# A hybrid decoder layer on one core: sums over a head's features, from float32 products to float32r products in two parts

## The chip, the core and the metric

The kernel runs on one core of one Trainium2 chip. The metric is device microseconds of one execution; lower is better. Before the change the median of three runs is 2262.58 us (2262.24 to 2262.78). Engines are named as in the profile: PE multiplies matrices and PEld is its weight load, DVE is the vector engine, ACT the scalar engine, POOL is GpSimd, and SP issues DMAs.

## The reference

One decoder layer on 256 tokens with 2048 features: a SwiGLU feed-forward block, a mixer, cross-attention to a memory, a second feed-forward block and a last norm. The mixer runs a sliding-window attention beside an RWKV-7 time mix of 16 heads with 64 features each, and merges them behind gates. The change touches three places of the time mix, each a sum or mean over the 64 features of a head:

```python
kk = k * k_k
kk = kk / jnp.maximum(jnp.sqrt(jnp.sum(kk * kk, axis=-1, keepdims=True)), 1e-12)   # 1
k = k * (1.0 + (a - 1.0) * k_a)
y = rwkv7_scan(r, decay, k, v, -kk, kk * a)
mean = jnp.mean(y, axis=-1, keepdims=True)
var = jnp.mean(jnp.square(y - mean), axis=-1, keepdims=True)                       # 3
y = ((y - mean) * lax.rsqrt(var + GN_EPS)).reshape(B, T, RWKV_WIDTH)
y = y * ln_w + ln_b
bonus = jnp.sum(r * k * r_k, axis=-1, keepdims=True) * v                           # 2
y = (y + bonus.reshape(B, T, RWKV_WIDTH)) * g
```

Everything is float32 in the reference, with the projections as plain products (`p = h @ w_in`, `y_attn @ w_proj_attn` and so on).

## The kernel before

**The weight stream.** The large products read 2048-feature weights in tiles of two k-tiles by 512 columns. SP issues their loads (`load`, L331) into the ring `raw` of four buffers. `split_unit` makes two float32r halves of a tile: ACT casts it to `hi` (L339) and DVE subtracts to get `lo` (L340), in rings of three. `times` (L412, L413, L414) then multiplies the activations' halves with them: high by hi, high by lo, low by hi, all float32r, accumulating in PSUM (`acc`). Such a tile with both token halves is an item: twelve products of 128x512. `next_item` splits items ahead of their use (AHEAD = 2).

**The work between.** Other work is written as generators, and an `Interleave` called `bg` advances them. `product` calls `bg.tick()` after each token half of an item, so there are two ticks an item. A tick advances the first generators of each group by one `yield`: const, feat, attn (two at once), ew (one at a time), chain (three), norm (one), mem. `idle(n)` yields n times. The time mix's steps are in these groups:

- `removal_keys(h)`, group ew, for each half h of the 16 heads: `kk`, its square `sq` (ACT, L1000), two products with `bdones` (L1005), square root (L1006), bound and reciprocal on DVE, then `kk` and `at` scaled. From these come 64-row products `kk` with `at` (L1042), in two groups c of eight, with the two row halves e in turn, each half into a PSUM bank of its own; DVE masks them to `lt` (L1048), POOL writes `lt` to a DRAM scratch `ld` (L1053).
- `substitute()`, group ew, behind both: SP reads `ld` back as `dl` in four transfers (L1063), and DVE solves a triangular system in small steps, `tmp` (L1070) and `xt` (L1075).
- `receptances(h)` and `values(h)`, group ew, later: the first forms the product r·k·r_k in `kt`; the second multiplies it with `bdones` (two products, L1131) for the bonus.
- `pair(h, j)`, group chain: the recurrence, for two heads at once.
- `finish(h, i)`, group norm, four in all: the square of `y`, a product with `bdmean` (L1273), square root (L1274), reciprocal, the group norm's scale and the gate.

`bdones` and `bdmean` are 128x128 float32 with two 64x64 blocks of 1 and of 1/64 on the diagonal, so that one product sums over the features of both heads in a tile and spreads the sum back over them. POOL makes them with memsets at the start of the mixer (L209 to L215). The sums go to PSUM banks `tr` (two).

**Around the change.** While `removal_keys` and `substitute` run, the foreground is four rounds of two products, w_in for a gate and then w_proj_attn (`ga`): ACT takes the sigmoid of the gate from PSUM (L1092), DVE multiplies the projection into it (L1095). During `receptances`, `values`, `pair` and `finish` the foreground is w_in for r and v and for the second gate, and then w_proj_rwkv.

**Memory and order.** The mixer's tiles of 4 KB for each partition come from one ring, `t4`, of N4 = 20 buffers; a tile that takes a buffer waits for the last use of the one before it. The instructions stand in each engine's queue in the order of the built program, which is not always the order of the source: a step whose operand comes late can stand behind later ones.

Of the kernel before, what the change touches and what calls it, by code (L numbers as in the profile page):

```python
# [8 lines left out]
F32R = mybir.dt.float32r  # L9
AF = mybir.ActivationFunctionType  # L10
ALU = mybir.AluOpType
# [4 lines left out]
P = 128  # L16
T = 256
# [12 lines left out]

UP, DOWN = 2.0**40, 2.0**-40
GROUPS = ((0, 4), (4, 4), (8, 3))
N4 = 20

AHEAD, LOADED = 2, 4

# [96 lines left out]
def decoder_layer(ctx: ExitStack, tc: tile.TileContext, a: dict, out: bass.AP):  # L133
    nc = tc.nc
    act, dve, pool, pe = nc.scalar, nc.vector, nc.gpsimd, nc.tensor
# [16 lines left out]
    def f32(x):  # L152
        return x.bitcast(F32)
# [7 lines left out]
    def tr():  # L161
        return ps.tile([P, 512], F32, tag="tr", name="tr", bufs=2)
# [5 lines left out]
    def idle(n):  # L168
        for _ in range(n):
            yield  # L170
# [20 lines left out]
    def mixer_constants(sp):  # L191

        abias = sp.tile([P, 2, P], F32, name="abias")
        pool.memset(abias[:], 0.0)
        select(abias[:, 0, :], abias[:, 0, :], [[1, P]], ALU.is_gt, NEG, 0, -1)
        select(abias[:, 1, :], abias[:, 1, :], [[-1, P]], ALU.is_ge, NEG, 0, 1)

        ups = sp.tile([P, 2, P], F32, name="ups")[:, 0, :]
        pool.memset(ups, UP)
        mask3 = sp.tile([P, 3, P], F32, name="mask3")  # L200
        select(mask3[:, 0, :], ups, [[1, P]], ALU.is_gt, 0.0, 0, -1)
        select(mask3[:, 1, :], ups, [[1, P]], ALU.is_ge, 0.0, 0, -1)
        select(mask3[:, 2, :], ups, [[1, P]], ALU.is_ge, 0.0, 0, -1)

        mask_l = sp.tile([P, P], F32, name="mask_l")
        select(mask_l[:], ups, [[-1, P]], ALU.is_gt, 0.0, 0, 1)
        bdones = sp.tile([P, P], F32, name="bdones")
        bdmean = sp.tile([P, P], F32, name="bdmean")
        pool.memset(bdones[:], 0.0)  # L209
        pool.memset(bdmean[:], 0.0)  # L210
        pool.memset(bdup, 0.0)
        for e in range(2):
            q = slice(64 * e, 64 * e + 64)
            pool.memset(bdones[q, q], 1.0)
            pool.memset(bdmean[q, q], 1.0 / 64)  # L215
            pool.memset(bdup[q, q], UP)
        pool.tensor_tensor(center[:], ident[:], bdmean[:], ALU.subtract)
        keep = sp.tile([P, 2, P], F32, name="keep")
        pool.memset(keep[:], 1.0)
        pool.memset(keep[:, :, 0:1], 0.0)  # L220
        return abias, mask3, mask_l, bdones, bdmean, keep

    sinks = cpool.tile([P, 16], F32, name="sinks")

# [41 lines left out]
    v = flat(a["rwkv_mu"])  # L266
# [462 lines left out]
    def aligned(sp):  # L729

        sp.tile([P, 16], F32, name="shift")
# [34 lines left out]

    with tc.tile_pool(name="mx", bufs=1, reuse_waits="tile") as sp:
        aligned(sp)
        abias, mask3, mask_l, bdones, bdmean, keep = mixer_constants(sp)

        def t4(name, shape=(P, 4, T), dt=F32):
            return sp.tile(list(shape), dt, tag="t4", name=name, bufs=N4)

# [10 lines left out]
            return s  # L784

        C4 = [0, P, 2 * P, 3 * P]


        def to_features(tok, dst, name):
            for q in (0, 2):  # L790
                act.copy(dst[:, q : q + 2, :], feat(tok, C4[q : q + 2]))
                yield
# [196 lines left out]
        kt = []  # L989

        def removal_keys(h):
            yield from wait_for(f"k{h}")
            yield from wait_for("decay")
            ei = cs[h]
            kk, sq = t4("kk"), t4("sq")
            for i in range(4):
                c = 4 * h + i
                act.activation(kk[:, i, :], kt[h][:, i, :], AF.Copy, scale=nk_k[:, c : c + 1])
            yield
            act.activation(sq[:], kk[:], AF.Square)  # L1000
            yield
            for i in (0, 2):
                b = tr()
                sq2 = sq[:, i : i + 2, :].rearrange("p c t -> p (c t)")
                pe.matmul(b[:], bdones[:], sq2, start=True, stop=True)  # L1005
                act.activation(sq2, b[:], AF.Sqrt)  # L1006
                yield
                dve.tensor_scalar(sq2, sq2, 1e-12, None, ALU.max)
                for k in range(2):
                    dve.reciprocal(sq[:, i + k, :], sq[:, i + k, :])  # L1010
                    yield from idle(2)
            dve.tensor_tensor(kk[:], kk[:], sq[:], ALU.mult)
            yield
            at_.append(t4("at"))
            for later, before in ((slice(1, P), ee[h][:, :, : P - 1]), (0, e0[h][:])):
                dve.scalar_tensor_tensor(
                    halves(at_[h])[:, :, later], halves(kk)[:, :, later], DOWN, before,
                    ALU.mult, ALU.mult,
                )
            yield  # L1020
            dve.scalar_tensor_tensor(kk[:], kk[:], -1.0, aa[h][:], ALU.mult, ALU.mult)
            yield
            dve.tensor_tensor(kk[:], kk[:], ei[:], ALU.mult)
            bt.append(kk)
            yield
            for i in range(4):
                c = 4 * h + i
                dve.tensor_scalar(
                    aa[h][:, i, :], aa[h][:, i, :], k_a[:, c : c + 1], ok_a[:, c : c + 1],
                    ALU.mult, ALU.add,  # L1030
                )
            pool.tensor_tensor(kt[h][:], kt[h][:], aa[h][:], ALU.mult)
            pool.tensor_tensor(aa[h][:], kt[h][:], ei[:], ALU.mult)

            for c in range(2):
                cs_ = slice(c * P, (c + 1) * P)
                lt = t4("lt", (P, 8, P))
                b = [mm() for _ in range(2)]
                for j in range(4):
                    for e in range(2):  # L1040
                        r = slice(64 * e, 64 * e + 64)
                        pe.matmul(  # L1042
                            b[e][:, j * P : (j + 1) * P], at_[h][r, j, cs_], bt[h][r, j, cs_],
                            start=True, stop=True,
                        )
                yield
                for e in range(2):
                    dve.tensor_tensor(  # L1048
                        lt[:, 4 * e : 4 * e + 4, :], b[e][:].rearrange("p (j s) -> p j s", j=4),
                        mask_l[:].unsqueeze(1).to_broadcast([P, 4, P]), ALU.mult,  # L1050
                    )
                o = h * 16 + c * 8
                pool.dma_start(ld[:, o : o + 8, :], lt[:])  # L1053
                yield
            yield
# [40 lines left out]
            pool.dma_start(blk(md, n), g[:])  # L1096


        rt, vtok, bv = [], [], []

        def receptances(h):
            yield from wait_for(f"r{h}")
            for i in range(4):
                c = 4 * h + i
                dve.scalar_tensor_tensor(
                    kt[h][:, i, :], rt[h][:, i, :], r_k[:, c : c + 1], kt[h][:, i, :],
                    ALU.mult, ALU.mult,
                )
                if i % 2:
                    yield  # L1110
            r3 = halves(rt[h])
            dve.scalar_tensor_tensor(r3, r3, DOWN, ee[h][:], ALU.mult, ALU.mult)
            yield

        def values(h):
            yield from wait_for(f"v{h}")
            vv = bv[h]
            vtok.append(t4("vtok", (P, 2, 512)))
            for c in range(2):
                b = tr()  # L1120

                for j in range(4):
                    pe.matmul(
                        b[:, j * P : (j + 1) * P], vv[:, j, c * P : (c + 1) * P], center[:],
                        start=True, stop=True,
                    )
                act.copy(vtok[h][:, c, :], b[:])
                yield
            for i in (0, 2):
                b = tr()  # L1130
                pe.matmul(  # L1131
                    b[:], bdones[:], kt[h][:, i : i + 2, :].rearrange("p c t -> p (c t)"),
                    start=True, stop=True,
                )
                v2 = vv[:, i : i + 2, :]
                dve.tensor_tensor(v2, b[:].rearrange("p (c t) -> p c t", c=2), v2, ALU.mult)
                yield
            bg.seen.add(f"ready{h}")
# [118 lines left out]
        def finish(h, i):  # L1257
# [10 lines left out]
            y = yq[h, i][:].rearrange("p c t -> p (c t)")  # L1268
            sq = sp.tile([P, 2 * T], F32, tag="sq", name="sq", bufs=1)
            act.activation(sq[:], y, AF.Square)  # L1270
            yield
            b = tr()
            pe.matmul(b[:], bdmean[:], sq[:], start=True, stop=True)  # L1273
            act.activation(sq[:], b[:], AF.Sqrt, bias=gneps[:])  # L1274
            yield
            dve.reciprocal(sq[:], sq[:])
# [1 line left out]
            b = tr()  # L1278
            for k in range(2):
                o = b[:, k * T : (k + 1) * T]  # L1280
                for m in range(2):
                    pe.matmul(
                        o, g2[:, m, k * P : (k + 1) * P], xg[:, m, :], start=k + m == 0,
                        stop=m == 1, **ek,
# [127 lines left out]
        for h in (0, 2):  # L1412
            b = tr()
# [17 lines left out]
    with tc.tile_pool(name="f2", bufs=1, reuse_waits="tile") as sp:  # L1431
# [37 lines left out]
        for t in range(2):  # L1469
            r = rstd(ss[:, t : t + 1, :])[0]  # L1470
# [42 lines left out]
```

## Time and profile before

| | before |
|---|---|
| median of three runs | 2262.58 us |
| the profiled execution | 2263.34 us |
| its span, first to last instruction | 2261.6 us |
| mean granted clock of PE | 0.999 |
| PE busy in 720 to 1600 us (mixer and cross-attention) | 877.28 of 880 us |
| DVE, ACT busy in the same stretch | 544.16 and 460.93 us |
| products with `bdones`, `bdmean` | 8 and 4, between 887.9 and 1278.4 us |

A float32 product of this kind leaves two records in the trace, so the twelve show as 24. Records of PE overlap, since products are pipelined; the distance between two starts tells what each took of PE. In a row of the timeline the columns are start and duration in us, engine, line, operation, output and inputs, and in brackets the idle time ahead of it with what ended it. A row of the chain of waits gives start, duration and what the chain's piece was. A row of one tile gives shortest, median and longest duration in ns. A row of the waits gives who waited for whom: us in total, times, longest.

### The profile page before, as it was taken

How to read it: one execution, taken by the hardware profiler on the slowest of the kernel's cores; microseconds unless marked ns; L12 is line 12 of the kernel's file. 1: busy time of each engine (PE TensorE's matmuls, PEld its weight loads, DVE VectorE, ACT ScalarE, POOL GpSimd, SP SyncE). 2: the span in 40 equal slices, each digit the busy share in tenths (PEclk: the TensorE clock that was granted, in tenths of full speed). 3: DMA queues.
4: the chain of work that ended last, by engine and by line, in shares of the span. 5: the costliest groups of instructions: out<-in, count | busy, mean ns of one | idle time of the engine just before them, and what ended most of it. 6: DMA issues, size and time to landing. Idle time of an engine off the chain costs nothing.

```text
span 2261.6 us, 28110 instructions
## 1 busy us (share of the span) xinstructions
PE 2246.8 (99%) x10617; PEld 1845.5 (82%) x10617; DVE 1778.4 (79%) x2281; ACT 1226.9 (54%) x1653; POOL 132.2 (6%) x192
## 2 busy tenths in 40 slices
PE   9999999999999999999999999999999999999998
PEld 7888888888888877788888888888888888888886
DVE  7899989998988477886434566547899988998987
ACT  6555555555556477444435446456555455555554
POOL 1000000000001000301220030001000000000002
PEclk9999999999999999999999999999999999999999
DMA  7555565555556544666433476647555565555564
GB/s 262 186 206 199 190 210 199 186 204 205 189 200 200 161 135 155 216 214 208 147 90 100 143 257 218 203 166 271 187 203 201 191 211 198 186 205 205 186 209 145
DMA packets 219144, 432.49 MB, mean 191 GB/s; under 512 B 14108, under 2 KB 16385, under 8 KB 219009
## 3 DMA queue, kind: packets, MB, share of 16 engines
q1 hardware_dynamic: 210432, 404.78, 52.7%
q0 software_dynamic: 8112, 25.12, 3.5%
q8 instruction: 83, 1.36, 0.2%
q10 hardware_dynamic: 464, 0.79, 0.1%
q14 instruction: 53, 0.43, 0.1%
HBM read 417.56 MB, written 13.11 MB: 190 GB/s over the span
## 4 chain that ended last, share of the span: by engine, by line
PE 96%; DVE 2%; issue 1%; DMA 1%; ACT 1%; SPq 0%; POOL 0%; POOLq 0%; DVEq 0%; ACTq 0%
PE acc L412 19%; PE acc L413 19%; PE acc L414 19%; PE mm L414 8%; PE mm L412 8%; PE mm L413 8%; PE tr L600 2%; PE tr L413 2%; PE tr L412 2%; PE tr L414 2%; PE mm L1212 1%; PE tr L1181 1%; DVE lo L340 1%; DMA raw<-in_w_out_dram 0%; PE mm L827 0%
## 5 line engine op out<-in xcount | busy, mean ns | idle before, releaser
L340 DVE TENSOR_TENSOR lo<-raw,hi 128x1024 fp32r<-128x1024 f32 (+1 forms) x770 | 894.0, 1163 | 352.9 <-ACT hi L339 351.2
L339 ACT CAST hi<-raw 128x1024 fp32r<-128x1024 f32 (+1 forms) x770 | 759.7, 997 | 747.5 <-PE acc L414 528.5
L412 PE MATMUL acc<-hi,xhi 128*128 128x512 f32 (+1 forms) x1196 | 477.7, 400 | 2.1 <-ACT xhi L627 1.7
L413 PE MATMUL acc<-lo,xhi 128*128 128x512 f32 (+1 forms) x1196 | 465.7, 389 | 0.0
L414 PE MATMUL acc<-hi,xlo 128*128 128x512 f32 (+1 forms) x1196 | 465.0, 389 | 0.0
L412 PEld LDWEIGHTS acc<-hi,xhi 128*128 128x128 f32 x1196 | 225.3, 188 | 52.1 <-issue 5.5
L413 PEld LDWEIGHTS acc<-lo,xhi 128*128 128x128 f32 x1196 | 225.2, 188 | 45.8 <-issue 3.2
L414 PEld LDWEIGHTS acc<-hi,xlo 128*128 128x128 f32 x1196 | 224.6, 188 | 46.5 <-DVE xlo L628 1.0
L347 ACT CAST thi<-raw 128x1024 fp32r<-128x1024 f32 x172 | 178.9, 1050 | 57.6 <-DVE raw L368 44.2
L348 DVE TENSOR_TENSOR tlo<-raw,thi 128x1024 fp32r<-128x1024 f32 x172 | 208.3, 1220 | 0.7 <-ACT thi L347 0.4
L412 PE MATMUL mm<-hi,xhi 128*128 128x512 f32 x380 | 149.5, 393 | 0.0
L414 PE MATMUL mm<-hi,xlo 128*128 128x512 f32 x380 | 148.3, 390 | 0.0
L413 PE MATMUL mm<-lo,xhi 128*128 128x512 f32 x380 | 148.3, 390 | 0.0
L413 PE MATMUL acc<-lo,hhi 128*128 128x512 f32 x372 | 145.7, 392 | 0.8 <-DVE lo L340 0.8
L414 PE MATMUL acc<-hi,hlo 128*128 128x512 f32 x372 | 145.7, 392 | 0.0
L412 PE MATMUL acc<-hi,hhi 128*128 128x512 f32 x372 | 145.1, 390 | 0.0
L414 PEld LDWEIGHTS mm<-hi,xlo 128*128 128x128 f32 x380 | 71.4, 188 | 15.0
L413 PEld LDWEIGHTS mm<-lo,xhi 128*128 128x128 f32 x380 | 71.4, 188 | 14.4
L412 PEld LDWEIGHTS mm<-hi,xhi 128*128 128x128 f32 x380 | 71.5, 188 | 14.4
L413 PEld LDWEIGHTS acc<-lo,hhi 128*128 128x128 f32 x372 | 69.9, 188 | 15.4 <-DVE lo L340 1.2
L412 PEld LDWEIGHTS acc<-hi,hhi 128*128 128x128 f32 x372 | 69.9, 188 | 14.3
L414 PEld LDWEIGHTS acc<-hi,hlo 128*128 128x128 f32 x372 | 70.0, 188 | 13.9
(384 smaller groups left out, 3550.2 us busy)
## 6 DMA issues: line engine op xcount, KB each, us to landing
raw<-in_ffn_w_up_dram SPq DMA_DIRECT2D x88, 1024.0 KB, 5.3
raw<-in_ffn_w_down_dram SPq DMA_DIRECT2D x88, 1024.0 KB, 5.1
raw<-in_ffn_w_gate_dram SPq DMA_DIRECT2D x84, 1024.0 KB, 5.1
raw<-in_w_in_dram SPq DMA_DIRECT2D x136, 512.0 KB, 3.5
raw<-in_w_out_dram SPq DMA_DIRECT2D x32, 512.0 KB, 4.4
raw<-in_w_proj_attn_dram SPq DMA_DIRECT2D x16, 512.0 KB, 3.8
raw<-in_w_proj_rwkv_dram SPq DMA_DIRECT2D x16, 512.0 KB, 5.9
raw<-in_w_cross_kv_dram SPq DMA_DIRECT2D x16, 512.0 KB, 3.7
```

What stands on the lines that cost most here:

```text
L339: at["hi"] = act.copy(hi[:, s], raw[:, s])
L340: at["lo"] = dve.tensor_tensor(lo[:, s], raw[:, s], f32(hi[:, s]), ALU.subtract)
L347: act.copy(hi[:], v[:])
L348: dve.tensor_tensor(lo[:], v[:], f32(hi[:]), ALU.subtract)
L412: pe.matmul(o, xh, hi, start=first, stop=False, **how)
L413: pe.matmul(o, xh, lo, start=False, stop=False, **how)
L414: pe.matmul(o, xl, hi, start=False, stop=last, **how)
L600: pe.transpose(b[:, o : o + P], tok[:, t, col : col + P], ident[:])
L1181: pe.matmul(b[e][:, m * P : (m + 1) * P], x1[r, j, cs_], x2[r, j, cs_], start=True, stop=True,)
L1212: pe.matmul(vb[:, o : o + P][:, r], lhs(e), rhs[:, r], start=first and e == 0, stop=True, **ek,)
```

## The change

The copies of the two constants in float32r are made on ACT, and the sums use these. The other factor is split into two float32r halves, the high one a copy on ACT, the low one a subtraction on DVE, and each sum becomes two accumulating products. For `removal_keys` the halves are `sh` and `sl`, for `values` `kh` and `kl` (made at the end of `receptances`), and for `finish` the two parts of `sp`. These are new tiles of the `t4` ring, which gets two buffers more. `removal_keys` and `finish` wait one tick longer ahead of the first sum, and `receptances` has one yield more.

```diff
-N4 = 20
+N4 = 22
...
-        return abias, mask3, mask_l, bdones, bdmean, keep
+        ones_r = []
+        for v in (bdones, bdmean):
+            r = sp.tile([P, P], F32R, name="ones_r" + str(len(ones_r)))
+            act.copy(r[:], v[:])
+            ones_r.append(r)
+        return abias, mask3, mask_l, ones_r, keep
...
+        def halves_of(v, hi, lo):
+            act.copy(hi, v)
+            dve.tensor_tensor(lo, v, f32(hi), ALU.subtract)
+            return hi, lo
+
+        def head_sums(ones_, v):
+
+            b = tr()
+            for i in range(2):
+                pe.matmul(b[:], ones_[:], v[i], start=i == 0, stop=i == 1)
+            return b
...
             act.activation(sq[:], kk[:], AF.Square)
-            yield
+            sp_ = halves_of(sq[:], t4("sh", dt=F32R)[:], t4("sl", dt=F32R)[:])
+            yield from idle(2)
             for i in (0, 2):
-                b = tr()
                 sq2 = sq[:, i : i + 2, :].rearrange("p c t -> p (c t)")
-                pe.matmul(b[:], bdones[:], sq2, start=True, stop=True)
+                b = head_sums(
+                    bdones, [v[:, i : i + 2, :].rearrange("p c t -> p (c t)") for v in sp_]
+                )
...
             dve.scalar_tensor_tensor(r3, r3, DOWN, ee[h][:], ALU.mult, ALU.mult)
             yield
+            kp.append(halves_of(kt[h][:], t4("kh", dt=F32R)[:], t4("kl", dt=F32R)[:]))
+            yield
...
-                b = tr()
-                pe.matmul(
-                    b[:], bdones[:], kt[h][:, i : i + 2, :].rearrange("p c t -> p (c t)"),
-                    start=True, stop=True,
+                b = head_sums(
+                    bdones, [v[:, i : i + 2, :].rearrange("p c t -> p (c t)") for v in kp[h]]
                 )
...
             act.activation(sq[:], y, AF.Square)
-            yield
-            b = tr()
-            pe.matmul(b[:], bdmean[:], sq[:], start=True, stop=True)
+            sp_ = t4("sp", (P, 2, 2 * T), dt=F32R)
+            sp_ = halves_of(sq[:], sp_[:, 0], sp_[:, 1])
+            yield from idle(2)
+            b = head_sums(bdmean, sp_)
```

Lines below the diff's edits have other numbers afterwards: L339 and L340 become L344 and L345, L412 to L414 become L417 to L419, L1042 L1061, L1048 L1067, L1063 L1082, L1092 and L1095 L1111 and L1114. The new sums are L802, their halves L794 and L795.

More of the change, by code (lines that the diff above doesn't have):

```diff
@@ L768, in decoder_layer @@
         aligned(sp)
-        abias, mask3, mask_l, bdones, bdmean, keep = mixer_constants(sp)
+        abias, mask3, mask_l, (bdones, bdmean), keep = mixer_constants(sp)
         def t4(name, shape=(P, 4, T), dt=F32):
@@ L1096, in decoder_layer @@
             pool.dma_start(blk(md, n), g[:])
-        rt, vtok, bv = [], [], []
+        rt, vtok, bv, kp = [], [], [], []
         def receptances(h):
```

## The prediction, made before the changed kernel ran

> **What bounds the kernel now.** I read the page's totals and its chain first, then the engines' busy time in stretches of 50 us around the changed lines, then what TensorE (PE) waited for there.
>
> ```profile
> span 2261.6 us, 28110 instructions
> PE 2246.8 (99%) x10617; PEld 1845.5 (82%) x10617; DVE 1778.4 (79%) x2281; ACT 1226.9 (54%) x1653; POOL 132.2 (6%) x192
> PE 96%; DVE 2%; issue 1%; DMA 1%; ACT 1%; SPq 0%; POOL 0%; POOLq 0%; DVEq 0%; ACTq 0%
> ...
> 900.00:950.00 50.00, 49.67 (x253) 39.42 (x252) 44.57 (x50) 25.92 (x30) 11.45 (x6) 1.00 0.61 194
> 950.00:1000.00 50.00, 50.00 (x222) 41.40 (x222) 37.37 (x66) 20.17 (x20) 7.11 (x8) 1.00 0.77 238
> 1150.00:1200.00 50.00, 50.00 (x326) 42.10 (x325) 20.93 (x26) 21.67 (x52) 6.45 (x11) 1.00 0.31 94
> 1250.00:1300.00 50.00, 49.77 (x280) 40.46 (x280) 24.02 (x26) 21.38 (x38) 2.16 (x3) 1.00 0.45 148
> ...
> PE tr L600 <- ACT tok L783: 0.8, 1, 0.8
> PE acc L412 <- DVE ga L1095: 0.4, 1, 0.4
> ...
> PE mm L1042 <- DVE lt L1048: 0.3, 1, 0.3
> ```
>
> The chain is PE for 96% of the span. The stretches (after the comma: PE, weight loads, DVE, ACT, POOL, clock, DMA) show PE full wherever the twelve matmuls stand; between 720 and 1600 us its longest wait is 0.8 us. So time taken from PE is time taken from the kernel, with no cover to lose, and any new lateness of a weight tile costs PE in full. Room on the others differs: in 900 to 950 us DVE is busy 44.6 of 50 us, in the later two stretches 21 to 24.
>
> **The sums themselves.** All twelve matmuls are 128x512; two records each.
>
> ```profile
> L1005 PE MATMUL tr<-sq,bdones x8: 589/592/592, 887.9 to 931.2; 128*128 128x512 f32 x8
> L1131 PE MATMUL tr<-kt,bdones x8: 590/592/596, 1098.1 to 1156.4; 128*128 128x512 f32 x8
> L1273 PE MATMUL tr<-sq,bdmean x8: 591/592/649, 1170.3 to 1278.4; 128*128 128x512 f32 x8
> ...
> 887.85 0.23 PE acc L414
> 888.08 0.86 PE tr L1005 x2
> 888.94 0.23 PE acc L412
> ...
> 1218.76 0.91 PE tr L1273 x2
> ```
>
> Durations overlap in the pipeline, so I price by the place in the chain: 0.86 us for the pair of records, 0.23 us for a float32r product of the same shape (the weight stream, L412 to L414). Two of those replace each: 0.86 − 0.46 = 0.40 us, and 12 × 0.40 = **−4.8 us**. The one extra weight load per sum (PEld) lies beside matmuls as the stream's loads do. Rows put the bounds at no gain (float32r with ones priced like float32, 2 × 0.43) and 12 × (0.91 − 0.45) = 5.5 us.
>
> **The ones in float32r.** Two copies join ACT's queue at the mixer's start and wait for POOL's memsets of the constants.
>
> ```profile
> 728.28 1.06 ACT L339 CAST hi<-raw 128x1024 fp32r<-128x1024 f32 x1 [1.25 <-PE acc L414]
> 731.00 1.05 ACT L339 CAST hi<-raw 128x1024 fp32r<-128x1024 f32 x1 [1.66 <-PE acc L414]
> ...
> 730.06 0.33 POOL L215 MEMSET bdmean<- 64x64 f32 x2
> ...
> 970.55 1.23 DVE L340 TENSOR_TENSOR lo<-raw,hi 128x1024 fp32r<-128x1024 f32 x1 [0.44 <-ACT hi L339]
> ```
>
> Behind them on ACT stands the weight stream's next cast. A weight item (two k-tiles, 12 products) takes 12 × 0.227 = 2.72 us of PE, which is also the distance of the two casts above, and the halves are made about two items ahead. The memsets end at 730.4; two small copies (under 0.3 us each, taken as a quarter of the 1.05 us for eight times the columns) end near 730.7; then cast and subtract, 1.06 + 1.23, are done near 733.0. PE wants that item two items after 728.2, at 733.65. Cost 0 with 0.6 us to spare; with the cover gone, the excess only.
>
> **Removal keys (L1005): the halves and the extra tick.**
>
> ```profile
> 884.96 1.06 ACT L1000 ACTIVATE sq<-kk 128x1024 f32<-128x1024 f32 x1
> 889.19 1.23 DVE L340 TENSOR_TENSOR lo<-raw,hi 128x1024 fp32r<-128x1024 f32 x1 [0.98 <-ACT hi L339]
> ```
>
> The new copy `sh` and subtract `sl` have the shape of the stream's cast and subtract: 1.05 us on ACT, 1.23 on DVE, for each of h = 0 and 1. In the order of the built program the sums come half an item later (1.4 us), and `sl` stands on DVE just ahead of the lo at 889.19. It would end at about 889.4 and its matmul comes at 889.7: 0 to 0.3 us per h, of which I take 0.
>
> What follows on DVE has no spare room (44.6 of 50) and decides a second thing, the 64-row products L1042:
>
> ```profile
> 910.50 1.38 DVE L1028 TENSOR_SCALAR aa<-aa,rv,ok_a 128x256 f32<-128x256 f32 x4
> 910.67 1.16 PE L1042 MATMUL mm<-kk,at 64*128 64x128 f32 x16
> 911.76 0.50 PE L414 MATMUL acc<-hi,yalo 128*128 128x512 f32 x1
> ...
> 913.67 1.16 PE L1042 MATMUL mm<-kk,at 64*128 64x128 f32 x14 [0.29 <-DVE lt L1048]
> 914.12 1.28 DVE L1095 TENSOR_TENSOR ga<-acc,ga 128x512 f32<-128x512 f32 x2
> 914.75 0.50 PE L412 MATMUL acc<-hi,xhi 128*128 128x512 f32 x1
> ...
> 945.70 1.16 PE L1042 MATMUL mm<-kk,at 64*128 64x128 f32 x16
> 946.79 0.51 PE L413 MATMUL acc<-lo,yahi 128*128 128x512 f32 x1
> ...
> 949.73 0.50 PE L412 MATMUL acc<-hi,yahi 128*128 128x512 f32 x1
> ```
>
> A group of eight products (16 records) takes 911.76 − 910.67 = 1.09 us while its two row halves alternate, e = 0 with e = 1. In the changed program the two groups of h stand together, with no stream products between, and the second is issued as four of e = 0, then four of e = 1, because the second PSUM bank comes free only with `lt`, and `lt` now stands on DVE behind four `aa` (1.38 us) and, for h = 0, a `ga` (half of 1.28). Four such products alone I estimate at 4 × 0.86/4 = 0.86 us, a quarter of the columns of the 0.86 us sum. For h = 0: `kk` done at 0, first group to 1.09, e = 0 to 1.95; `aa`, `ga`, `lt` (shaped like `ga`) to 1.38 + 0.64 + 0.64 = 2.66; e = 1 to 3.5. Before, from 910.67 to 914.75 with five stream products (1.14) between, it was 2.94: **+0.55**. For h = 1 no `ga` is ahead, the bank is freed at 1.38 + 0.64 = 2.0, with the hand-over 2.1, and e = 1 ends near 3.0; before, from 945.70 to 949.73 with six stream products (1.37) between, it was 2.65: **+0.35**. Together **+0.9**, from 0 (pairing and waits as before) to 2 (both waits a `ga` longer).
>
> [...]
>
> **One weight item late (w_proj_attn, second column block).** The shift moves the rest of that queue about 1.2 items later, and with it the four reads `dl<-ld` (L1063) on SP and the fifteen small steps of `substitute` (L1070, L1075) on DVE. SP's queue also carries the weight loads. In the built program one load more goes ahead of these reads, and the first load of this product now goes behind all four.
>
> ```profile
> 958.90 4.39 SPq L1063 DMA_DIRECT2D dl<-ld x4
> 964.00 6.50 SPq L331 DMA_DIRECT2D raw<-in_w_proj_attn_dram  x4
> dl<-ld SPq DMA_DIRECT2D x4, 128.0 KB, 4.7
> ...
> 969.47 1.05 ACT L339 CAST hi<-raw 128x1024 fp32r<-128x1024 f32 x1 [0.61 <-DMA raw<-in_w_proj_attn_dram]
> 973.47 0.69 ACT L1092 ACTIVATE ga<-acc,rs 128x512 f32<-128x512 f32 x1 [0.59 <-PE acc L414]
> 974.54 0.69 ACT L1092 ACTIVATE ga<-acc,rs 128x512 f32<-128x512 f32 x1 [0.39 <-PE acc L414]
> 975.13 1.04 ACT L339 CAST hi<-raw 128x1024 fp32r<-128x1024 f32 x1
> ```
>
> Before, the cast at 969.47 took that load, two instructions ahead of the gate activations `ga` (L1092). In the changed program ACT has both `ga` first and that cast behind them. The second `ga` needs the last product of the item before; so the cast starts only when PE has run out of products. From 973.47 and 974.54 I place that last product's end near 974.35: 0.19 us until ACT starts, 0.59 from there to the cast (974.54 to 975.13), 1.05 for it, 0.05 back to PE (an estimate). The first product is 1.88 us late. Two products can go on the hi half (0.46); the third needs lo: 1.23 more. It is late by 1.88 + 1.23 − 0.46 ≈ **+2.7 us**. Bounds: 0 (if the cast gets past) and 4.5 (if lo also finds the fifteen steps unfinished). By position this is the only place in the mixer where the margin falls from 12 or 13 products to one.
>
> [...]
>
> **What is hidden.** `kh` and `kl` (once per h) and the four `sp` pairs come where DVE and ACT are busy 21 to 24 of 50 us, a whole item or more ahead of their sums. Two rings more (N4 22) only take waits away, on POOL. The last steps of `finish` come about two items later, with their users over five items behind. Reordering in the pair chain may shift a wait either way: ±1.5 us, taken as 0.
>
> **Sum.** −4.8 + 0.9 + 2.7 = −1.2 us. The profiled execution took 2263.34 us, 1.7 over its span and 0.76 over the median: 2262.1 in its frame, **2261.4** against the median of 2262.58. About 0.2% (4.5 us) is what a measurement of this kernel can tell from no change.
>
> **The rivals.** *Full saving*: the stall and the lost pairing are covered after all, by ACT reaching the cast early and by `lt` going before `ga`; −4.8 gives 2257.8. For it: PE is the bound and −4.8 is straight from rows. Against: the program's order at both places. Chance 0.24; little more than half of it falls beyond 0.2%, as 4.8 barely passes 4.5. *Late reads (slower)*: the fifteen steps cannot start before the fourth `dl` read has landed, and lo stands behind them. Before, the reads were issued from 958.9 to 963.3, so with 4.7 us to land the last came in near 968. With 1.2 items' shift (3.2 us) I expect 971.2; the steps, 3.3 us, end at 974.5, against 976.4 when lo could start. The price is landing − 973.1: from 978.8, 7.6 us later than I expect, it adds 5.7 us and the sum becomes +4.5, 2267.1. For it: DMA is at 0.77 of its capacity there, the highest of the stretches. Against: it would take a landing of 12 us, against the 4.7 of the row. Chance 0.12. *It doesn't do what it says*: float32r sums priced like float32; +0.9 + 2.7 = +3.6, 2266.2. The stream's 0.23 us for the same shape speaks against it: 0.06. *My sum*: 0.58, its own range −3 to +1.5 us.
>
> **How the numbers follow.** The range takes the sum, the larger part of the full saving, and reaches up to the third rival: 2257.6 to 2266.4; outside lie the late reads (0.12) and a third of the full saving (0.08). Faster by over 0.2% (below 2258.1): 0.15, from the full saving and a little of the sum. Slower by over 0.2% (above 2267.1): 0.14, the late reads and a third of the chance that float32r saves nothing. The rest, 0.71, is within.
>
> **What would show it.** In the chain after, each sum should be two places of 0.23 us with no wait ahead of it; ones copies near 730 and no PE wait behind them; the two groups of the 64-row products side by side, with a wait for `lt` in the second; a PE wait of about 1.9 us, then one of 0.8 to 1.0, at the second w_proj_attn product near 972 us, named <-ACT hi and <-DVE lo. No wait there, or waits of a like size elsewhere (the pair chain, 1090 to 1300 us), would make the forecast wrong; sums of 0.43 us a half, too.

## The result

The changed kernel takes 2265.44 us (median of 20 runs, 2264.05 to 2266.99), the kernel before 2262.47 us (2262.13 to 2263.37): 3.0 us slower, a ratio of 1.0014 with an interval of 1.0007 to 1.002. The forecast was 1.2 us faster. The time lies inside the range and within 0.2%, but on the other side.

The page of the changed kernel; its profiled execution took 2266.94 us, among the slowest of the 20:

```profile
span 2265.2 us, 28127 instructions
PE 2247.4 (99%) x10617; PEld 1847.8 (82%) x10617; DVE 1784.4 (79%) x2289; ACT 1236.7 (55%) x1665; POOL 132.1 (6%) x192
PE 94%; DVE 3%; issue 1%; DMA 1%; ACT 0%; POOL 0%; POOLq 0%; ACTq 0%; DVEq 0%
```

PE holds 94% of the chain, against 96 before, and its busy time has not fallen although twelve products of 0.86 us are gone. What PE waited for between 720 and 1600 us in the changed kernel:

```profile
PE acc L417 <- ACT hi L344: 1.7, 1, 1.7
PE tr L605 <- DVE x L1374: 1.1, 2, 0.8
PE tr L605 <- ACT tok L788: 0.8, 1, 0.8
PE mm L1061 <- DVE lt L1067: 0.6, 2, 0.4
PE acc L418 <- DVE lo L345: 0.5, 1, 0.5
```

The first and the last row are the wait that the prediction placed at the second w_proj_attn product. Waits alone don't give the account, so I compared the start of the same weight-stream product in both traces (both have 8958, so the n-th can be set beside the n-th). The difference moves only at these places (the eight sums of the pair chain's stretch are put at the price of the first four):

```
place (before, us)           after - before   terms
885 to 936, four sums        -1.80            4 x -0.45
909 to 955, L1061 (h=0, 1)   +0.35, +0.75     64-row products
973 to 980, late item        +4.45            1.7 + 0.5 wait, the rest see below
1015 to 1089                 -0.13
1089 to 1292, pair chain     -0.72            8 x -0.45 = -3.6, so +2.9 lost
1372 to 1378, w_out          +0.91            wait for x
start +0.11, after 1570      -0.35
sum                          +3.57
```

The late item and the clock. These are the SP, ACT and PE rows of the timeline of the changed kernel, then the chain of waits behind them:

```profile
964.31 2.50 SPq L1082 DMA_DIRECT2D dl<-ld  x4
966.91 2.32 SPq L336 DMA_DIRECT2D raw<-in_w_proj_attn_dram  x4
...
972.60 0.69 ACT L1111 ACTIVATE ga<-acc,rs 128x512 f32<-128x512 f32 x1 [5.75 <-PE acc L419]
973.96 0.69 ACT L1111 ACTIVATE ga<-acc,rs 128x512 f32<-128x512 f32 x1 [0.67 <-PE acc L419]
974.55 2.93 ACT L344 CAST hi<-raw 128x1024 fp32r<-128x1024 f32 x3
...
975.63 0.73 PE L417 MATMUL acc<-hi,yahi 128*128 128x512 f32 x2 [1.71 <-ACT hi L344]
976.89 0.50 PE L418 MATMUL acc<-lo,yahi 128*128 128x512 f32 x1 [0.53 <-DVE lo L345]
```

```profile
977.62 0.23 PE acc L417
977.86 0.41 PE acc L418
978.26 0.43 PE acc L419
...
980.83 0.43 PE acc L417
981.25 0.25 PE acc L418
981.50 0.23 PE acc L419
```

Both `ga` stand ahead of the cast, the cast starts after the second, and PE waits 1.71 and then 0.53 us. Just behind, eight products take 0.41 to 0.43 us each in place of 0.23, from 977.86 to 981.25. That is the PE clock, as the stretches (clock after the POOL column) show for the changed kernel and then for before:

```profile
975.00:980.00 5.00, 3.84 (x11) 2.79 (x12) 4.32 (x8) 2.47 (x3) 0.00 (x0) 0.77 0.41 121
980.00:985.00 5.00, 5.00 (x20) 4.01 (x20) 3.18 (x9) 2.10 (x2) 0.00 (x0) 0.88 0.83 227
```

```profile
975.00:980.00 5.00, 5.00 (x23) 4.13 (x22) 3.77 (x11) 2.24 (x4) 0.00 (x0) 1.00 0.65 200
```

In finer stretches of the changed kernel the clock is 0.51 from 977.9 to 981.2 us and 1.00 from 981.3 us: 8 × 0.2 = 1.6 us on top of the wait's 2.8. This profiled execution had the drop and so stands in the slower half of the 20; without the 1.6 the table's sum is +2.0.

### The profile page after: what moved, and what is told of

Read it like the earlier page. It is cut to its first block, busy times and chain, and to the rows that moved or that the text cites. A ratio compares the mean times of both kernels' runs of the same rounds, so it can differ in the third digit from the quotient of the medians.

```text
span 2265.2 us, 28127 instructions
## 1 busy us (share of the span) xinstructions
PE 2247.4 (99%) x10617; PEld 1847.8 (82%) x10617; DVE 1784.4 (79%) x2289; ACT 1236.7 (55%) x1665; POOL 132.1 (6%) x192
## 4 chain that ended last, share of the span: by engine, by line
PE 94%; DVE 3%; issue 1%; DMA 1%; ACT 0%; POOL 0%; POOLq 0%; ACTq 0%; DVEq 0%
PE acc L417 19%; PE acc L418 19%; PE acc L419 19%; PE mm L419 8%; PE mm L418 8%; PE mm L417 8%; PE tr L605 2%; PE tr L418 2%; PE tr L417 2%; PE tr L419 2%; DVE lo L345 1%; PE mm L1231 1%; PE tr L1200 1%; DMA raw<-in_w_out_dram 0%; PE mm L844 0%
## 5 line engine op out<-in xcount | busy, mean ns | idle before, releaser
L345 DVE TENSOR_TENSOR lo<-raw,hi 128x1024 fp32r<-128x1024 f32 (+1 forms) x770 | 893.8, 1163 | 342.4 <-ACT hi L344 340.6
L344 ACT CAST hi<-raw 128x1024 fp32r<-128x1024 f32 (+1 forms) x770 | 759.2, 997 | 723.1 <-PE acc L419 510.4
L417 PE MATMUL acc<-hi,xhi 128*128 128x512 f32 (+1 forms) x1196 | 474.4, 397 | 1.8 <-ACT xhi L632 1.5
L419 PE MATMUL acc<-hi,xlo 128*128 128x512 f32 (+1 forms) x1196 | 464.5, 389 | 0.0
L417 PEld LDWEIGHTS acc<-hi,xhi 128*128 128x128 f32 x1196 | 225.4, 188 | 50.1 <-issue 3.2
L419 PEld LDWEIGHTS acc<-hi,xlo 128*128 128x128 f32 x1196 | 224.8, 188 | 46.5 <-issue 0.3
L417 PE MATMUL mm<-hi,xhi 128*128 128x512 f32 x380 | 149.3, 393 | 0.0
L419 PE MATMUL mm<-hi,xlo 128*128 128x512 f32 x380 | 148.1, 390 | 0.0
L419 PE MATMUL acc<-hi,hlo 128*128 128x512 f32 x372 | 145.5, 391 | 0.0
L417 PE MATMUL acc<-hi,hhi 128*128 128x512 f32 x372 | 144.9, 390 | 0.0
L419 PEld LDWEIGHTS mm<-hi,xlo 128*128 128x128 f32 x380 | 71.3, 188 | 15.0
L417 PEld LDWEIGHTS mm<-hi,xhi 128*128 128x128 f32 x380 | 71.4, 188 | 14.5
L417 PEld LDWEIGHTS acc<-hi,hhi 128*128 128x128 f32 x372 | 69.9, 188 | 14.3
L419 PEld LDWEIGHTS acc<-hi,hlo 128*128 128x128 f32 x372 | 69.9, 188 | 13.9
```

The lines of the kernel that those rows point to most:

```text
L344: at["hi"] = act.copy(hi[:, s], raw[:, s])
L345: at["lo"] = dve.tensor_tensor(lo[:, s], raw[:, s], f32(hi[:, s]), ALU.subtract)
L417: pe.matmul(o, xh, hi, start=first, stop=False, **how)
L419: pe.matmul(o, xl, hi, start=False, stop=last, **how)
```

## The experiments

All are timed beside the kernel before on the same chip (2262.35 to 2262.38 us there). Theory A: the extra tick in `removal_keys`, not the new work, makes the weight item late. Each rival is in the expectations.

**Only the sums of removal_keys.** The other eight sums stay as they were; their halves and extra yields go back too, in lines not shown here.

```diff
-                b = head_sums(bdones, [... for v in kp[h]])      # values
+                pe.matmul(b[:], bdones_f[:], kt[h]..., start=True, stop=True)
...
-            b = head_sums(bdmean, sp_)                            # finish
+            pe.matmul(b[:], bdmean_f[:], sq[:], start=True, stop=True)
```

> Only the sums of removal_keys (four of the twelve) go to float32r, with their halves and the extra tick; the eight sums of values and finish stay float32 products. From the trace of the changed kernel, counted at the weight stream's products against those of before: four sums -1.8 us, the 64-row products +1.1, the late weight item of the second w_proj_attn product +4.45 (1.7 us waiting for hi, 0.5 for lo, the rest in products that took 0.43 us each while the granted clock was down). Theory A (the loss sits in removal_keys alone): +3.7, near 2266.2, and the stretch of the pair chain runs as before. Rival B (the shift of removal_keys also reorders the pair chain, where another 2.9 us were lost): near +6.6, 2269.

Measured: 2267.19 us (2266.63 to 2268.62), +4.8, between the two. By the same comparison of starts: sums −1.8, L1061 +1.1, late item +2.8, and the pair chain's stretch +1.7 although nothing in it was edited. So part of that loss comes from the shift. The late item costs 2.8 here, not 4.45; the PE rows of its timeline and the stretch after them say why:

```profile
975.25 0.73 PE L417 MATMUL acc<-hi,yahi 128*128 128x512 f32 x2 [1.71 <-ACT hi L344]
976.51 0.50 PE L418 MATMUL acc<-lo,yahi 128*128 128x512 f32 x1 [0.53 <-DVE lo L345]
```

```profile
975.00:980.00 5.00, 4.22 (x17) 3.21 (x18) 4.67 (x9) 2.97 (x4) 0.00 (x0) 1.00 0.42 120
```

The same two waits, 1.71 and 0.53, and the clock stayed at 1.00. The drop is not certain: with this wait it came in three of the four profiled executions that had it (the changed kernel, the third and the sixth run). It also fits the spread of the changed kernel's 20 runs: ten with a mean clock of 0.999 average 2264.8 us and ten with 0.998 average 2266.4, 1.6 apart. In the kernel before, the same two clock means go with times that differ by at most 0.1 us (2262.33 against 2262.46, 2262.39 against 2262.41).

**Only the other eight sums.** `removal_keys` as before, with no tick more.

```diff
-            sp_ = halves_of(sq[:], t4("sh", dt=F32R)[:], t4("sl", dt=F32R)[:])
-            yield from idle(2)
+            yield
...
+                pe.matmul(b[:], bdones_f[:], sq2, start=True, stop=True)
```

> The other eight sums (values, finish) go to float32r, removal_keys stays as before. Theory A: no late weight item, no clock drop near 975 us, no change at the 64-row products; the eight sums give -3.6, the pair chain takes back 2.9 and the wait for x after it 0.9 if their reordering comes from the edits in receptances and finish: +0.2, 2262.7. Rival B (the pair chain's loss came from the shift of removal_keys): -3.6, 2258.9.

Measured: 2259.29 us (2258.84 to 2259.98), −3.1, ratio 0.9986 (0.9977 to 0.9995): rival B. The pair chain's stretch gains 4.0, more than the 3.6 of the sums; the wait for x takes 0.8 back. So the edits in `receptances` and `finish` don't cost the 2.9 us by themselves. The shift of `removal_keys` by itself cost 1.7 in the first run; the rest comes only where both are together.

**The tick alone.** The kernel before with `yield` made `yield from idle(2)` in `removal_keys`, nothing else.

```diff
             act.activation(sq[:], kk[:], AF.Square)
-            yield
+            yield from idle(2)
```

> The kernel before with one edit: removal_keys waits one tick longer ahead of its first sum (twice in all). No halves, no float32r ones, all sums float32. Theory A (the tick moves the reads of substitute past a weight load on SP and the gate activations past a cast on ACT): the late weight item appears as in the changed kernel, +4.4 with the clock drop, and up to +1 at the 64-row products: 2266.9 to 2268. Rival C (the new work on ACT and DVE delays that item): no wait there, 2262.5.

Measured: 2267.99 us (2266.32 to 2268.84), +5.6, Theory A. The trace has the late item (1.7 and 0.5 us of wait, clock 0.76 and 0.90 in the two stretches of 975 to 985 us, +4.3 in all), and +1.4 in the pair chain's stretch. All with float32 sums and no halves: rival C falls.

**The change without the tick.**

```diff
             sp_ = halves_of(sq[:], t4("sh", dt=F32R)[:], t4("sl", dt=F32R)[:])
-            yield from idle(2)
+            yield
```

> The changed kernel without the extra tick in removal_keys; all twelve sums in float32r, all halves. Theory A: no late weight item and no clock drop near 975 us: the changed kernel's 2265.4 less 4.45, about 2261.0; the sums of removal_keys may wait up to 1 us each for their low half, as it is made half an item ahead of them at most: up to 2262. Rival C (the halves' work makes the item late): the wait stays, 2265.

Measured: 2258.37 us (2257.51 to 2259.16), −4.0, ratio 0.9982 (0.9973 to 0.9991), better than expected, since the pair chain's loss goes as well: its stretch gains 3.95. The low halves of the second h cost 0.3 us of wait.

**The reads on another queue.** The change as it is, tick too.

```diff
-                nc.sync.dma_start(dl[q], ld[q, :, q].rearrange("t h s -> h t s"))
+                pool.dma_start(dl[q], ld[q, :, q].rearrange("t h s -> h t s"))
```

> The changed kernel, tick and all, with one edit: the four reads of ld into dl (L1082) are issued by POOL in place of SP. In the built program the pair chain's products stand in the same order as in the changed kernel, and the cast of the second w_proj_attn product now stands ahead of both gate activations on ACT. Theory A (these reads ahead of the weight loads in SP's queue make that item late): the wait there and the clock drop behind it go, 2.8 to 4.4 us: 2261.0 to 2262.6. Rival D (the tick makes it late by itself, whichever queue reads): the wait stays, 2265.

Measured: 2263.14 us (2260.77 to 2265.28), ratio 1.0003 (0.9994 to 1.0012). ACT's timeline and a PE wait of this run:

```profile
971.30 1.05 ACT L344 CAST hi<-raw 128x1024 fp32r<-128x1024 f32 x1 [1.67 <-PE acc L419]
972.66 0.69 ACT L1111 ACTIVATE ga<-acc,rs 128x512 f32<-128x512 f32 x1 [0.31 <-PE acc L419]
974.02 0.69 ACT L1111 ACTIVATE ga<-acc,rs 128x512 f32<-128x512 f32 x1 [0.67 <-PE acc L419]
```

```profile
PE acc L417 <- DVE ga L1114: 1.2, 1, 1.2
```

The cast is ahead of the gates, the wait and the clock drop at 975 us are gone (0.0 there by the starts, clock 1.00 from 970 to 985 us), and the rest is as in the changed kernel. A new wait of 1.2 us, 1.5 by the starts, for the product of gate and projection comes some items later, so 2.3 us are gained, not 2.8 to 4.4. With the tick in place, then, the item is late only while the reads stand on SP's queue: rival D falls. The edit changes two things at once, the cast's place on ACT and the issue of the loads (the product's first one at 960.0 us, against 966.9 in the changed kernel), and so doesn't tell which of them the wait came from; the landing of that load, further down, speaks for the place on ACT. Why DVE is late in the new place I did not follow up.

**The solve one tick earlier.** The change as it is, but for `substitute`. Here Theory E is tested: the pair chain's loss is products of the two row halves that no longer stand next to each other.

```diff
         def substitute():
-            yield from idle(4)
+            yield from idle(3)
```

> The changed kernel with substitute waiting three ticks instead of four at its start; the late weight item keeps its place in the order. In the built program the 64-row products of the pair chain change their row half between neighbours 40 times in the stretch of the pair chain, against 23 in the changed kernel and 29 before. Theory E (the pair chain's loss is products of the two row halves that no longer stand side by side): from the traces so far each further change of half is worth 1.8 overlapping products of 0.144 us, so 17 x 0.26 = -4.4 us: near 2261, with the 1.7 us wait for hi still there. Rival F (the loss there is waits, or more switches between the weight stream and the chain): within 1 us of 2265.4.

Measured: 2260.19 us (2259.05 to 2263.31), 5.2 less than the changed kernel, with the late item still in it (+4.15 in the profiled execution, clock drop included; that execution was the slowest of the 11). The pair chain's stretch is 5.3 us shorter than in the changed kernel. Its groups of 64-row products in the stretch of 1085 to 1300 us (count, then busy time and mean ns), before, in the changed kernel, and in this run:

```profile
L1181 PE MATMUL tr<-at,aa 64*128 64x128 f32 x64 | 13.0, 323 | 0.0
L1181 PE MATMUL tr<-rt,aa 64*128 64x128 f32 x64 | 10.4, 272 | 0.0
L1181 PE MATMUL tr<-rt,kk 64*128 64x128 f32 x64 | 10.4, 272 | 0.0
```

```profile
L1200 PE MATMUL tr<-at,aa 64*128 64x128 f32 x64 | 13.5, 322 | 0.0
L1200 PE MATMUL tr<-rt,aa 64*128 64x128 f32 x64 | 10.9, 274 | 0.0
L1200 PE MATMUL tr<-rt,kk 64*128 64x128 f32 x64 | 10.8, 272 | 0.0
```

```profile
L1200 PE MATMUL tr<-at,aa 64*128 64x128 f32 x64 | 12.2, 323 | 0.0
L1200 PE MATMUL tr<-rt,aa 64*128 64x128 f32 x64 | 9.9, 272 | 0.0
L1200 PE MATMUL tr<-rt,kk 64*128 64x128 f32 x64 | 9.9, 272 | 0.0
```

The same 64 records of the same mean length are busy for 33.8, 35.2 and 32.0 us, because more or fewer of them lie over one another. Counted in the traces, products that start less than 0.02 us ahead of the next number 97 before, 86 in the changed kernel, 109 here, and 104 in the two runs without the tick; the background products of the stretch, from the start of each to the next start and without the sums, take 94.6, 96.3, 92.2 and 93.7 us. Between the changed kernel and this run that is 0.18 us for each overlap, a rough price: from before to the changed kernel it is 0.15, and between other pairs of runs it goes from 0.13 to 0.4. The remaining 1.1 us lie in the products of the weight stream, which PE leaves for the chain on six fewer occasions; what one such switch costs was not tested by itself. So Theory E holds for most of it, and rival F for a part.

**No tick, and the solve later.**

```diff
-            yield from idle(2)         # removal_keys, ahead of the sums
+            yield
...
-            yield from idle(4)         # substitute
+            yield from idle(5)
```

> All twelve sums in float32r, no extra tick in removal_keys, substitute waiting five ticks in place of four. No late weight item in the order; 40 changes of row half in the pair chain against 33 in the run without the key tick, five switches fewer. Theory E: 7 x 0.26 = -1.8 and up to -0.5 for the switches against 2258.4: 2256.1 to 2256.6. Rival F: 2258.4.

Measured: 2257.02 us (2256.45 to 2257.89), −5.3, ratio 0.9976 (0.9967 to 0.9985). Overlapping products 108, background 92.2 us. That is 1.35 us less than the run without the tick, where Theory E gave 1.8 to 2.3 and rival F nothing. This is the fastest version, faster than both kernels.

**The kernel before, solve earlier.**

```diff
-            yield from idle(4)         # substitute
+            yield from idle(3)
```

> The kernel before, all sums float32, with substitute waiting three ticks in place of four: 39 changes of row half against 29. Theory E: 10 x 0.26 = -2.6 with no part of the change in it: near 2259.8. Rival F: 2262.4.

Measured: 2260.66 us (2260.3 to 2261.45), −1.7 against −2.6 expected, ratio 0.9993 (0.9984 to 1.0002). The interval reaches no change, but all 11 times lie below all 32 of the kernel before beside them (2261.91 to 2263.01). Overlapping products 107, background 93.0 us, and 1.6 us off the stretch. So a gain a third as large as the best version's can be had without float32r. Between this run and the one above, with nearly as many overlaps, the change without its tick is worth 3.6 us.

## Why the prediction was wrong

**The step that failed** is "Reordering in the pair chain may shift a wait either way: ±1.5 us, taken as 0". It cost 2.9 us, outside its bounds, and it was no wait: 1.7 us of it is lost overlap of the background products (94.6 to 96.3), the rest lies in the weight stream's products, which PE leaves for the chain on four more occasions. I had priced just this loss of overlap at the 64-row products of `removal_keys`, and let the same products in `pair` go as hidden. Three runs show it: the tick alone loses 1.4 us there with none of the edits in that stretch, the change without the tick loses nothing, and moving `substitute` by one tick wins 5.3 back. From the forecast −1.2 to the +3.6 of the profiled execution it is the largest term; the others are the clock drop (+1.6), the wait for x (+0.9), the 64-row products (+0.2), the late item (+0.1), the sums (−0.6) and small shifts elsewhere (−0.4).

**The late item** came as forecast in place and size: waits of 1.7 and 0.5 us (1.9 and 0.8 to 1.0 in the forecast), 2.8 by the starts, against 2.7. What was missing is the clock of 0.51 behind it, 1.6 us in part of the executions; the bound of 4.5 happened to hold it, for another reason. By the trace the order on ACT was the cause, as forecast. The product's first load, held up behind the four `dl` reads, was issued at 966.91 us in the changed kernel and landed 5.7 us later, near 972.6, two us ahead of its cast; ACT sat idle for 0.67 us before the second `ga` meanwhile. The chain has ACT going from the second `ga` to the cast without a DMA between:

```profile
973.70 0.24 PE acc L419
...
973.96 0.02 ACT ga L1111
...
974.55 1.04 ACT hi L344
...
975.61 1.24 DVE lo L345
```

From the second `ga` to the cast it is 0.59 us, just as before the change (974.54 to 975.13). Started at the landing, the cast would have ended near 973.65, ahead of the 973.94 at which PE ran out, and only lo would have been late, by some 0.5 us: an estimate from these rows, not a run.

**The sums** gave a little more than I took: −0.45 us each by the starts for the four of `removal_keys`, against −0.40. At that price for all twelve it is −5.4. Taken from the distances around each of the other eight, these gave 0.36 to 0.45, about 3.3 us together; then the twelve make −5.1, against −4.8, and the loss in the pair chain's stretch is 2.6 us, still outside its bounds. The rows of the ones' tile in the changed kernel:

```profile
L802 PE MATMUL tr<-sh,ones_r x4: 389/389/389, 889.4 to 932.6; 128*128 128x512 f32 x4
L802 PE MATMUL tr<-sl,ones_r x4: 389/389/389, 889.8 to 932.8; 128*128 128x512 f32 x4
```

They are exactly as long as a weight-stream product, 0.39 us with the overlap, 0.23 from start to start, and the low half is there in time. A float32r sum priced like a float32 one is ruled out.

**The 64-row products** of `removal_keys` cost 1.1 us by the starts, against 0.9, but not in the forecast shares: 0.35 for h = 0 in place of 0.55, and 0.75 for h = 1 in place of 0.35. That the sum fits is in part luck. For h = 0 the order is the forecast one:

```profile
912.59 2.05 PE L1061 MATMUL mm<-kk,at 64*128 64x128 f32 x24
915.05 1.16 PE L1061 MATMUL mm<-kk,at 64*128 64x128 f32 x8 [0.41 <-DVE lt L1067]
916.13 0.50 PE L417 MATMUL acc<-hi,xhi 128*128 128x512 f32 x1
```

From 912.59 to 916.13 it is 3.54 us, forecast 3.5.

**The ones** cost nothing at the start, as forecast: the copies came at 730.20 and 730.58, and the start comparison doesn't move there.

```profile
730.20 0.30 ACT L224 CAST ones_r<-bdones 128x128 fp32r<-128x128 f32 x1 [3.01 <-POOL bdones L214]
730.58 0.30 ACT L224 CAST ones_r<-bdmean 128x128 fp32r<-128x128 f32 x1
```

**Not foreseen at all** was the wait for x near 1375 us (PE tr L605, 1.1 us in place of 0.3), some 80 us behind the last edited step. In the runs it goes from a gain of 0.5 to a loss of 3.0 us (clock drop included). Why the DVE step before it is late there was not settled.

**The rivals.** The full saving, −4.8, comes near for the change without its tick: −4.0, after the wait for x takes 0.7 back there. The late reads did not come: `tmp` began at 970.09 us in the changed kernel, the fifteen steps ahead of lo were done before lo could start. (The 976.4 at which the prediction lets lo start is 976.2 by its own terms; that changes nothing.)

## What to carry to other kernels

Where background steps are interleaved by ticks, one tick more is a change of its own: it moved the time by 5.6 us without any change of the arithmetic, more than the twelve cheaper products were worth. So time the tick alone beside the edit, and look after it at every queue that the moved steps share, here SP's loads behind `dl` and ACT's cast behind `ga`. Products on half the rows took their time from who stood next to them: from 912.59 us on in the changed kernel, sixteen records of `removal_keys` with the two row halves in turn took 1.0 us, and the eight of one half behind them 0.9 us. So after a reordering count how many overlap, in every stretch downstream of it; and try a tick more or less at a neutral place before judging the edit.

## What the runs showed of the hardware

Behind a wait of 1.71 us on PE, followed by one of 0.53, the granted clock was 0.51 for 3.4 us in the changed kernel, at a price of 1.6 us; three of four profiled executions with these waits showed such a drop, and one did not (clock 1.00). Shorter waits had one behind them too. At the start of the changed kernel PE waited 1.54 us for xhi, until 7.91 us, and the clock was 0.50 from 8.5 to 11.8 us; the kernel before waited 0.77 and 0.88 us for it there, with the clock at 1.00. In the run with the solve a tick earlier PE waited 1.4 us for x near 1374 us; its row of the waits and then of the chain:

```profile
PE tr L605 <- DVE x L1374: 1.7, 2, 1.4
```

```profile
1375.37 0.32 PE acc L417
1375.69 0.43 PE acc L418
...
1378.68 0.34 PE acc L417
1379.02 0.23 PE acc L418
```

From 1375.4 to 1378.8 the products take 0.43 us again, 3.4 us long. The wait of 1.2 us in the run with the reads on POOL cost 1.5 us by the starts, which leaves no room for a drop of 1.6. The times of kernels with such waits also spread more, 2.9 us in the changed kernel and 4.3 in the sixth run against 1.2 in the kernel before, but not in step with them: 2.0 in the first run, which has the same waits as the changed kernel, and 4.5 in the fifth, whose profiled execution has none above 1.2 us between 700 and 1600 us.
